# A two-branch attention block: the fourth query tile's turning transfer in two pieces, and the sums of exponentials scaled with one tensor input

## The chip, the cores and the metric

The kernel runs on one core of one Trainium2 chip. The metric is the device time of one execution in microseconds (us), from the first to the last thing that the core does. A core has a matrix engine (TensorE, PE in the profile), whose weight loads are shown apart (PEld), a vector engine (VectorE, DVE), an engine for functions of single elements (ScalarE, ACT), a general engine (GpSimd, POOL) and one that issues transfers (SyncE, SP). Transfers run on 16 DMA engines. Every transfer of this kernel is issued by SP, one after the other.

## What is computed

The reference is one decoder layer with two attention branches beside each other, cut here to what the change concerns (512 tokens behind 16 learned ones, 16 heads in each branch, all in float32):

```python
def attend(qb, qpos, cq=None):                     # one block of 128 queries
    s = jnp.einsum('bhqd,bhkd->bhqk', qb, k) * scale
    if cq is not None:                             # the second branch: forget gates, summed up
        s = s + (cq[..., :, None] - cum[:, :, None, :])
    s = jnp.where(key_pos[None, :] <= qpos[:, None], s, -jnp.inf)
    p = jax.nn.softmax(s, axis=-1)
    return jnp.einsum('bhqk,bhkd->bhqd', p, v)
...
o_mla = causal_block_attention(q_m, k_m, v_mla, MLA_SCALE)
y_mla = (o_mla * jax.nn.silu(z_mla)) @ w_br_mla
o_fox = causal_block_attention(fox_heads(fq), fox_heads(fk), fox_heads(fv), FOX_SCALE, cum)
y_fox = (o_fox * jax.nn.silu(z_fox)) @ w_br_fox
mixed = (jax.nn.sigmoid(gate_a) * y_mla + jax.nn.sigmoid(gate_b) * y_fox) @ w_out
return (h + rmsnorm(mixed, post_norm_g))[:, N_META:]
```

## The kernel before

**The whole.** First the tokens are normalised and turned, and the small projections are made. Then comes the attention in 16 stages, and then gates, branch products and the output product. Products are made in two or three passes over high and low halves of the numbers, so that they come out near float32.

**A stage.** A stage handles two heads of one branch: `stages` (L1121) goes over eight pairs of heads, FoX (`br` 1) and MLA (`br` 0) in turn. Stages are counted from 0 here, so the even ones are FoX. What a stage does is in `attention` (L938):

- `scores()` (L985): TensorE makes the scores of the four query tiles b = 0 to 3 (128 queries each, tile b with 144 + 128 b keys). VectorE takes them out of PSUM with mask or bias and row maximum (L979), and ScalarE makes the exponentials in place, each with its row sum in `su` (L1014).
- `norm(0)` for tiles 0 to 2 and `norm(1)` for tile 3 (L1021): `inverse` (L1017) multiplies the sums by 1/512 and takes reciprocals (`ri`). GpSimd writes the 16 learned tokens' probabilities (L1034 to L1039), ScalarE the high halves of the others (L1049), VectorE the low halves (L1053), all in float16 into `pn`. One transfer for each tile then turns it (keys to the partitions) into `pt` (L1072). Tile b has 2b + 3 columns of tiles, each for two heads, so the four transfers move 6, 10, 14 and 18 squares of 128 by 128.
- `values()` (L1079): 26 matmuls of `pt` by the turned values `vp` into one bank: two for the learned tokens (512 queries wide), then six for each key block j of 0 to 3, over the queries from 128 j on.

**How stages overlap.** The order of TensorE's work is the order in which the program is written (the manual schedule of L725). The loop at L1248 writes the scores of a stage, then `values()` of the stage before (`late`), then the projections for the next stage (`fill`: `fq`, `fk`, `v`, `z`, `mq`, `mk`), with `norm` written in between. So while TensorE goes through some 20 us of projections, the other engines and the transfers bring the probabilities of the stage to their place, and `values()` stands behind the next stage's scores. VectorE, ScalarE, GpSimd and SP get their order from the scheduler of the language, by priorities and dependences. It also spreads the transfers over eight completion semaphores in turn.

**SP's queue around it.** Beside the turning transfers it has the weight loads of coming stages (`wraw`), the bias rows (`cbp`), the stored and reloaded rotary part of the queries (`qpe_dram`, `QP`) and the turning of the values (`vp`). `dma` (L95) issues all of them through the same queue.

The lines that the change touches are in `inverse` and in the last loop of `norm`'s `fn`:

Of the kernel before, what the change touches and what calls it, by code (L numbers as in the profile page):

```python
# [17 lines left out]
ALU = mybir.AluOpType  # L18
# [22 lines left out]
PSCALE = 512.0  # L41
# [15 lines left out]
def block_kernel(ctx: ExitStack, tc: tile.TileContext, x, meta_tokens, pre_norm_g, w_in, fox_forget_b,  # L57
                 mla_q_norm_g, mla_kv_norm_g, w_uq, w_ukv, w_br_mla, w_br_fox, w_out, post_norm_g,
                 rope_tok, rope_pe, out):
    nc = tc.nc  # L60
# [21 lines left out]
    su = const.tile([128, 64], F32, tag="su", name="su")  # L82
# [12 lines left out]
    def dma(out, src, start=None):  # L95

        with tc.issue_after(sums_out[0]) if written[0] and sums_out else nullcontext():
            ins = (start or nc.sync.dma_start)(out=out, in_=src)
        if written[0]:
            tc.keep_in_program_order(ins)  # L100
        return ins.ins
# [300 lines left out]
    with ExitStack() as ph:  # L402
# [294 lines left out]
        with tc.issue_after(lowered[("k", 1, 0), 1]):  # L697
            nc.vector.tensor_tensor_scan(out=fa[:, 0], data0=fa[:, 1], data1=fa[:, 2], initial=0.0, op0=ALU.add,
                                         op1=ALU.add)
# [8 lines left out]
    def gate_unit(room=None, own=False):  # L708

        i, br = gates.pop(0)  # L710
        off = (O_GA, O_GB)[br]
        w, act = (plain_w(off, i), both_act) if own else (win_w(off, i, room), u_act)

        def done(_, ps):
            if len(ths) % 7 > 4:
                ths[i, br] = thx[0].tile([128, S], F32, tag="thx", name=f"th{i}{br}")
            else:
                ths[i, br] = thp.tile([128, L], F32, tag="th", name=f"th{i}{br}")[:, 0:S]
            nc.scalar.activation(ths[i, br], ps, AF.Tanh, scale=w.r)
        return unit(f"pg{i}{br}", w, act, KD, REAL, done)  # L720


    with ExitStack() as att:
# [31 lines left out]
        pn = [ac.tile([128, n, 2, 128], F16, tag=f"pn{g}", name=f"pn{g}") for g, n in enumerate((17, 9))]  # L755

        ptt = ac.tile([128, 18, 512], F16, tag="pt", name="pt")
# [8 lines left out]
        masks, normed, whole, turned_p, between = [], [], [], [], []  # L766
# [171 lines left out]
        def attention(br, pr):  # L938
# [18 lines left out]
            def sf_of(h, b):  # L957
                o, n = SF_STEP * (b % 3), 144 + 128 * b
                return sfs[b // 3][:, h, o : o + n]
# [12 lines left out]
            def evict(places):  # L972
                for b, c0, w, o, ps in places:
                    for h in range(2):
                        nb = sums["nb"][:, h, b : b + 1]
                        for a, e, in1 in added(h, b, c0, c0 + w):

                            with tc.high_priority(offset=100):
                                ins = nc.vector.tensor_tensor_reduce(  # L979
                                    out=sf_of(h, b)[:, a:e], in0=ps[h][:, o + a - c0 : o + e - c0],  # L980
                                    in1=in1, scale=-scale, scalar=3.0e38 if a == 0 else nb,
                                    op0=ALU.add, op1=ALU.min, accum_out=nb)
                return ins.ins
# [25 lines left out]
            def exponentials(bs):  # L1009
                with tc.high_priority(offset=60):  # L1010
                    for b in bs:
                        for h in range(2):
                            sf = sf_of(h, b)
                            exps[b // 3] = nc.scalar.activation(sf, sf, AF.Exp, bias=sums["nb"][:, h, b : b + 1],  # L1014
                                                                scale=-1.0, accum_out=sums["su"][:, h, b : b + 1]).ins

            def inverse(su, ri):  # L1017
                nc.vector.scalar_tensor_tensor(out=su, in0=su, scalar=1.0 / PSCALE, in1=su, op0=ALU.mult, op1=ALU.min)
                return nc.vector.reciprocal(ri, su).ins  # L1019

            def norm(g):  # L1021
                def fn():
                    b0, nb_ = GRP[g][0], len(GRP[g])
                    su, ri = (sums[t][:, :, b0 : b0 + nb_] for t in ("su", "ri"))
                    if not (three_first and g):
                        inv = inverse(su, ri)
                    if three_first and g == 0:
                        with tc.issue_after(inv):
                            evict([p_ for p_ in places if p_[0] == 3])

                    mt = aw.tile([128, 2, nb_, META], F32, tag=f"mt{g}", name=f"mt{nm_}{g}", bufs=1)
                    src = sfs[g][:, :, 0 : SF_STEP * nb_].rearrange("p h (b c) -> p h b c", b=nb_)[:, :, :, 0:META]
                    dst = pn[g][:, 0 : PN_STEP * nb_].rearrange("p (b t) h c -> p h b t c", b=nb_)[:, :, :, 0]
                    nc.gpsimd.tensor_tensor(out=mt, in0=src, in1=ri.unsqueeze(3).broadcast_to([128, 2, nb_, META]),  # L1034
                                            op=ALU.mult)
                    hi, lo, hi2 = (dst[:, :, :, 32 * i : 32 * i + META] for i in range(3))
                    nc.gpsimd.tensor_copy(hi, mt)
                    lead[:] = lead[-1:] + [nc.gpsimd.tensor_tensor(out=lo, in0=mt, in1=hi, op=ALU.subtract).ins]
                    nc.gpsimd.tensor_copy(hi2, mt)  # L1039
                    def parts(b, h):  # L1040
                        sf = sf_of(h, b)[:, META:].rearrange("p (j c) -> p j c", c=128)
                        t0 = PN_STEP * (b % 3) + 1
                        hi, lo = (pn[g][:, t0 : t0 + 2 * b + 2, h].rearrange("p (j l) c -> p j l c", l=2)[:, :, i]
                                  for i in range(2))
                        return sf, hi, lo, sums["ri"][:, h, b : b + 1]

                    def high(b, h):
                        sf, hi, _, rib = parts(b, h)
                        normed[:] = [nc.scalar.activation(hi, sf, AF.Copy, scale=rib).ins]  # L1049

                    def lower(b, h):
                        sf, hi, lo, rib = parts(b, h)
                        nc.vector.scalar_tensor_tensor(out=lo, in0=sf, scalar=rib, in1=hi, op0=ALU.mult, op1=ALU.subtract)  # L1053

                    early = three_first and g == 0
                    for b in GRP[g]:
                        if early and b == GRP[g][-1]:
                            for h in range(2):
                                high(b, h)
                            with tc.issue_after(normed[0]):  # L1060
                                exponentials((3,))
                            inv = inverse(*(sums[t][:, :, 3:4] for t in ("su", "ri")))
                            with tc.issue_after(inv):
                                for h in range(2):
                                    lower(b, h)
                            continue
                        for h in range(2):
                            high(b, h)
                            lower(b, h)
                    for b in GRP[g]:  # L1070
                        t0, n = PN_STEP * (b % 3), 2 * b + 3
                        turned_p[:] = [dma(ptt[:, 0 : 2 * n, 128 * b : 128 * b + 128], pn[g][:, t0 : t0 + n].rearrange("p t h c -> p (t h c)"),  # L1072
                                           nc.sync.dma_start_transpose)]
                        if between and b == 1:
                            with tc.issue_after(turned_p[0]):
                                between.pop()()
                return fn
# [62 lines left out]
        g = gate_unit(own=True)  # L1140
# [209 lines left out]
    with ExitStack() as mg:  # L1350
# [169 lines left out]
        for i in range(HK):  # L1520
            at, n = False, 0
# [190 lines left out]
```

## Time and profile before

| | |
|---|---|
| median of 3 runs | 580.1 us (579.19 to 581.66) |
| the profiled execution: its time | 580.54 us |
| its span, first to last instruction | 578.8 us |
| granted TensorE clock | 0.995 |
| TensorE busy | 563.0 us of the span, 3864 matmuls |
| VectorE, ScalarE, GpSimd busy | 468.0, 390.8, 232.1 us |
| moved by the DMA engines | 97.74 MB in 220025 packets |

The profile shows one execution on the chip. Times are us from the span's start, durations of single instructions are ns where a column says so. In a row such as `L104 PE MATMUL ov<-pt,vp`, L104 is the line of the kernel (here a helper through which all matmuls go), and `ov<-pt,vp` names what is written and read, without buffer numbers. In a timeline the bracket at a row's end is the engine's idle time before it and what ended it; neighbouring instructions of one kind stand in one row (x4). SPq is SP's queue: its times are those of issuing, not of moving. In the chain of waits each row starts at the time in its first column, and a row `DMA pt<-pn` reaches from the issue of a transfer to its landing.

### The profile page before, as it was taken

The numbers are of one execution on the slowest core, as the hardware profiler recorded it, in microseconds if no ns is written. First come the engines' busy times: TensorE is split into PE (matmuls) and PEld (weight loads), VectorE is DVE, ScalarE is ACT, GpSimd is POOL, SyncE is SP. The second block draws the span as 40 slices with busy tenths as digits, with TensorE's granted clock in tenths as the row PEclk, the third lists the DMA queues.
The fourth block names the chain that finished last, engine by engine and source line by source line (L and its number), as shares of the span: only waits on it lengthen the run. The fifth ranks groups of instructions, "written<-read, shape, count | busy, mean of one in ns | idle before, by whom it ended". The sixth has DMA issues, their size and how long they took to land.

```text
span 578.8 us, 11317 instructions
## 1 busy us (share of the span) xinstructions
PE 563.0 (97%) x3864; PEld 399.8 (69%) x3864; DVE 468.0 (81%) x1251; ACT 390.8 (68%) x859; POOL 232.1 (40%) x346
## 2 busy tenths in 40 slices
PE   8999979999999999999999999999999999999995
PEld 6888656667568668567676676645686675788884
DVE  6868798888878989878888788879958986478966
ACT  7867787787885886976887878864443463343762
POOL 4422823775685597756846756600000000000000
PEclk9999998999999999999999999999999999999999
DMA  8525899889999897997997986658824230323603
GB/s 301 106 56 152 254 175 290 161 210 241 193 223 220 156 200 132 217 228 150 244 247 162 211 183 146 156 102 295 286 74 110 72 110 11 110 99 109 219 0 145
DMA packets 220025, 97.74 MB, mean 169 GB/s; under 512 B 131352, under 2 KB 209568, under 8 KB 219968
## 3 DMA queue, kind: packets, MB, share of 16 engines
q1 hardware_dynamic: 219968, 97.03, 70.1%
q8 instruction: 30, 0.49, 0.3%
q14 instruction: 27, 0.22, 0.1%
HBM read 62.62 MB, written 4.23 MB: 116 GB/s over the span
## 4 chain that ended last, share of the span: by engine, by line
PE 77%; DVE 8%; DMA 5%; ACT 4%; issue 2%; POOL 2%; SPq 1%; DVEq 0%; ACTq 0%; POOLq 0%
PE z L104 15%; PE pg L104 10%; PE py L104 8%; PE fq L104 7%; PE v L104 7%; PE x L104 6%; PE fk L104 6%; PE st L104 5%; PE ov L104 5%; DMA pt<-pn 4%; PE psm L104 2%; PE mq L104 2%; PE y L104 2%; DVE w L269 1%; DVE wl L110 1%
## 5 line engine op out<-in xcount | busy, mean ns | idle before, releaser
L104 PEld LDWEIGHTS <-w 128*128 128x128 f16 x1584 | 150.1, 98 | 114.6 <-issue 4.3
L1014 ACT ACTIVATE sf<-sf,nb 128x272 f32<-128x272 f32 (+3 forms) x128 | 72.7, 568 | 25.3 <-DVE nb L979 23.1
L104 PE MATMUL z<-hTh,w 128*128 128x512 f16 x256 | 81.9, 380 | 0.0
L272 POOL TENSOR_TENSOR w<-wraw,w 128x1024 f16<-128x1024 f32 x35 | 74.9, 2141 | 2.3
L104 PE MATMUL pg<-hTh,w 128*128 128x512 f16 x240 | 72.6, 379 | 0.8 <-DVE w L269 0.8
L1053 DVE SCALAR_TENSOR_TENSOR pn<-sf,ri,pn 128x512 f16<-128x512 f32 (+3 forms) x128 | 70.9, 611 | 1.6 <-ACT pn L1049 1.6
L219 POOL TENSOR_SCALAR sc<-sc,su 128x2 f32<-128x2 f32 (+2 forms) x22 | 8.3, 379 | 146.3 <-DVE sc L216 146.3
L258 ACT ACTIVATE w<-wraw,sc 128x1024 f16<-128x1024 f32 x43 | 48.3, 1144 | 24.2 <-DVE sc L218 18.5
L1049 ACT ACTIVATE pn<-sf,ri 128x128 f16<-128x128 f32 (+3 forms) x128 | 59.6, 547 | 0.5 <-DVE ri L1019 0.5
L104 PE MATMUL z<-hTl,w 128*128 128x512 f16 x128 | 48.5, 379 | 0.0
L110 DVE TENSOR_TENSOR wl<-wraw,w 128x512 fp32r<-128x512 f32 (+1 forms) x44 | 38.4, 880 | 12.2 <-PE scale L104 4.4
L271 POOL TENSOR_SCALAR wraw<-wraw,sc 128x1024 f32<-128x1024 f32 x35 | 39.8, 1136 | 20.5 <-ACT w L258 19.4
L104 PE MATMUL pg<-hTl,w 128*128 128x512 f16 x120 | 45.5, 379 | 0.0
L104 PE MATMUL st<-hlk,hlq 64*128 64x272 f32 (+4 forms) x480 | 41.4, 299 | 0.0
L104 PE MATMUL fk<-hTh,w 128*128 128x272 f16 (+1 forms) x224 | 40.1, 276 | 0.0
L104 PE MATMUL v<-hTh,w 128*128 128x272 f16 (+1 forms) x224 | 39.3, 276 | 0.0
L104 PE MATMUL ov<-pt,vp 128*64 128x512 f16 (+4 forms) x416 | 33.2, 311 | 4.7 <-DMA pt<-pn 4.7
L104 PEld LDWEIGHTS st<-hlk,hlq 64*128 64x128 f32 x480 | 33.1, 186 | 5.8 <-ACT vh L903 2.5
L104 PE MATMUL fq<-hTh,w 128*128 128x512 f16 x112 | 35.2, 386 | 0.0
L104 PEld LDWEIGHTS <-vp 128*64 128x64 f16 (+1 forms) x416 | 22.3, 111 | 17.7 <-issue 6.9
L1415 ACT CAST w<-wraw 128x512 fp32r<-128x512 f32 x28 | 16.7, 617 | 23.1 <-DVE wraw L1424 18.6
L165 ACT CAST w<-wraw 128x1024 fp32r<-128x1024 f32 (+1 forms) x20 | 20.2, 1015 | 17.0 <-PE py L104 15.3
(342 smaller groups left out, 1478.5 us busy)
## 6 DMA issues: line engine op xcount, KB each, us to landing
wraw<-in_w_in_dram SPq DMA_DIRECT2D x47, 512.0 KB
room<-in_w_in_dram SPq DMA_DIRECT2D x9, 512.0 KB
cbp<-c_dram SPq DMA_DIRECT2D x16, 264.0 KB
wraw<-in_w_br_fox_dram SPq DMA_DIRECT2D x8, 512.0 KB
tb<-in_w_out_dram SPq DMA_DIRECT2D x8, 512.0 KB
wraw<-in_w_br_mla_dram SPq DMA_DIRECT2D x8, 512.0 KB
wraw<-in_w_out_dram SPq DMA_DIRECT2D x6, 512.0 KB
QP<-qpe_dram SPq DMA_DIRECT2D x8, 256.0 KB
```

Of the source, the lines that this page charges most:

```text
L104: nc.tensor.matmul(*a, **k)
L110: return eng.tensor_tensor(out=lo, in0=src, in1=f32(hi), op=ALU.subtract)
L165: nc.scalar.copy(wh[:, :n], raw[:, :n])
L219: nc.gpsimd.tensor_scalar(out=r, in0=t, scalar1=su[:, 5:6], scalar2=1.0, op0=ALU.mult, op1=ALU.mult)
L258: self.hi = nc.scalar.activation(hi, raw, AF.Copy, scale=self.s).ins
L269: nc.vector.scalar_tensor_tensor(out=lo, in0=raw, scalar=self.s, in1=hi, op0=ALU.mult, op1=ALU.subtract)
L271: nc.gpsimd.tensor_scalar(out=raw, in0=raw, scalar1=self.s, scalar2=1.0, op0=ALU.mult, op1=ALU.mult)
L272: nc.gpsimd.tensor_tensor(out=lo, in0=raw, in1=hi, op=ALU.subtract)
L1014: exps[b // 3] = nc.scalar.activation(sf, sf, AF.Exp, bias=sums["nb"][:, h, b : b + 1], scale=-1.0, accum_out=sums["su"][:, h, b : b + 1]).ins
L1049: normed[:] = [nc.scalar.activation(hi, sf, AF.Copy, scale=rib).ins]
L1053: nc.vector.scalar_tensor_tensor(out=lo, in0=sf, scalar=rib, in1=hi, op0=ALU.mult, op1=ALU.subtract)
L1415: nc.scalar.copy(to[0], src)
```

## The change

There are two edits, both in `attention`.

```diff
             def inverse(su, ri):
-                nc.vector.scalar_tensor_tensor(out=su, in0=su, scalar=1.0 / PSCALE, in1=su, op0=ALU.mult, op1=ALU.min)
+                su_ = su.rearrange("p h b -> p b h")
+                nc.vector.tensor_scalar(out=su_, in0=su_, scalar1=1.0 / PSCALE, scalar2=None, op0=ALU.mult)
                 return nc.vector.reciprocal(ri, su).ins
...
                     for b in GRP[g]:
                         t0, n = PN_STEP * (b % 3), 2 * b + 3
-                        turned_p[:] = [dma(ptt[:, 0 : 2 * n, 128 * b : 128 * b + 128], pn[g][:, t0 : t0 + n].rearrange("p t h c -> p (t h c)"),
-                                           nc.sync.dma_start_transpose)]
+                        for t, m in ((0, 5), (5, 4)) if b == 3 else ((0, n),):
+                            turned_p[:] = [dma(ptt[:, 2 * t : 2 * (t + m), 128 * b : 128 * b + 128],
+                                               pn[g][:, t0 + t : t0 + t + m].rearrange("p t h c -> p (t h c)"), nc.sync.dma_start_transpose)]
```

**The transfer.** Tile 3's 18 squares go in two transfers, a first piece of 10 (learned tokens and key blocks 0 and 1) and a second of 8 (key blocks 2 and 3). That is 16 more transfers in the kernel. What waited for the last turning transfer (`turned_p`) now waits for the second piece.

In the FoX stages and in stage 1 the two pieces stand where the one transfer stood. SP's queue in stage 4, before; `pn_757` is tile 3's buffer, and the last figures are partitions x squares x columns:

```order
L1103 DMA cbp_745<-c_dram 128x528
L98 DMA_TRANSPOSE pt<-pn_756 128x6x128
L98 DMA_TRANSPOSE pt<-pn_756 128x10x128
L98 DMA_TRANSPOSE pt<-pn_756 128x14x128
L98 DMA_TRANSPOSE pt<-pn_757 128x18x128
L98 DMA wraw_2354<-in_w_in_dram 128x8x128
```

and now (SP's queue, the same place):

```order
L1105 DMA cbp_745<-c_dram 128x528
L98 DMA_TRANSPOSE pt<-pn_756 128x6x128
L98 DMA_TRANSPOSE pt<-pn_756 128x10x128
L98 DMA_TRANSPOSE pt<-pn_756 128x14x128
L98 DMA_TRANSPOSE pt<-pn_757 128x10x128
L98 DMA_TRANSPOSE pt<-pn_757 128x8x128
L98 DMA wraw_2359<-in_w_in_dram 128x8x128
```

Only the last transfer of the four is cut, and nothing else moves.

In the seven MLA stages from stage 3 on, the scheduler had put tile 3's transfer second. SP's queue in stage 5, before:

```order
L98 DMA QP<-qpe_dram 128x512
L98 DMA_TRANSPOSE pt<-pn_756 128x6x128
L98 DMA_TRANSPOSE pt<-pn_757 128x18x128
L98 DMA_TRANSPOSE pt<-pn_756 128x10x128
L98 DMA_TRANSPOSE pt<-pn_756 128x14x128
L98 DMA wraw_3082<-in_w_in_dram 128x8x128
```

and now (SP's queue in stage 5):

```order
L98 DMA QP<-qpe_dram 128x512
L98 DMA_TRANSPOSE pt<-pn_756 128x6x128
L98 DMA_TRANSPOSE pt<-pn_757 128x10x128
L98 DMA_TRANSPOSE pt<-pn_756 128x10x128
L98 DMA_TRANSPOSE pt<-pn_756 128x14x128
L98 DMA_TRANSPOSE pt<-pn_757 128x8x128
L98 DMA wraw_3089<-in_w_in_dram 128x8x128
```

The second piece has moved behind tiles 1 and 2. Outside of the turning transfers the order of every engine's instructions is as it was. TensorE gains a wait: the 15th of the 26 matmuls of `values()`, the first of key block 2, waits for the second piece; the first matmul waits for the others.

**The sums.** The instruction that scales `su` read it as two tensors (times 1/512, then the minimum with itself, which is the same as the product, the sums being positive). It now reads it once, and walks it with the tiles outside and the heads inside (3 by 2 elements for tiles 0 to 2, and 2 elements for tile 3). There are 32 of them, as before.

## The prediction

> **What bounds the kernel now.** I read the page first, its table of engines and its chain of waits:
>
> ```profile
> PE 563.0 (97%) x3864; PEld 399.8 (69%) x3864; DVE 468.0 (81%) x1251; ACT 390.8 (68%) x859; POOL 232.1 (40%) x346
> ...
> PE 77%; DVE 8%; DMA 5%; ACT 4%; issue 2%; POOL 2%; SPq 1%; DVEq 0%; ACTq 0%; POOLq 0%
> ```
>
> TensorE is busy for 97% of the span and carries 77% of the chain. Nothing in the change takes work off it, so the change can gain only where TensorE waits. The waits of TensorE, longest first (sum in us, how often, the longest), say how much that is:
>
> ```profile
> PE ov L104 <- DMA pt<-pn: 4.7, 4, 2.4
> PE spun L104 <- DVE KPL L371: 1.5, 1, 1.5
> PE pg L104 <- DVE w L269: 0.8, 2, 0.4
> ```
>
> The largest wait is the one that the change touches: `values()` waits for the turning transfers, in 4 of 16 stages, 4.7 us together. All others are short and elsewhere. So 4.7 us is the most that the split can win if nothing else moves. The chain of waits in order of time shows the four places, and TensorE's timeline what each costs:
>
> ```profile
> 80.21 6.31 DMA pt<-pn
> ...
> 142.63 5.86 DMA pt<-pn
> ...
> 243.39 5.86 DMA pt<-pn
> ...
> 284.06 5.17 DMA pt<-pn
> ```
>
> ```profile
> 86.66 2.66 PE L104 MATMUL ov<-pt,vp 80*64 80x512 f16 x26 [2.42 <-DMA pt<-pn]
> ```
> ```profile
> 148.63 2.04 PE L104 MATMUL ov<-pt,vp 80*64 80x512 f16 x26 [0.86 <-DMA pt<-pn]
> ```
> ```profile
> 249.39 1.87 PE L104 MATMUL ov<-pt,vp 80*64 80x512 f16 x20 [0.70 <-DMA pt<-pn]
> ```
> ```profile
> 289.37 2.04 PE L104 MATMUL ov<-pt,vp 80*64 80x512 f16 x26 [0.76 <-DMA pt<-pn]
> ```
>
> These are stages 0, 3, 8 and 10. In each the last transfer of the stage lands (80.21 + 6.31 = 86.52, and so on) 0.14 us before the first matmul starts. In the other twelve stages TensorE finds its probabilities there.
>
> How busy the transfers are, by stretches (us, busy time of PE, PEld, DVE, ACT, POOL with counts, clock, DMA share, GB/s):
>
> ```profile
> 62.00:370.00 308.00, 302.40 (x2425) 206.10 (x2424) 256.63 (x866) 242.16 (x568) 202.80 (x293) 0.99 0.94 201
> 370.00:579.00 209.00, 201.45 (x1088) 142.78 (x1085) 165.19 (x248) 102.78 (x167) 5.52 (x14) 0.99 0.41 125
> ```
>
> In the attention the DMA engines are as full as TensorE (share 0.94), behind it not at all (0.41). So the transfers of a stage form a burst that runs at the DMA engines' pace, and the end of that burst meets `values()`.
>
> **The split, in the nine stages where the pieces stand last** (0, 8 and 10 of those that wait). SP's queue has the four transfers of a stage in one row, here stages 2, 3 and 8:
>
> ```profile
> 115.97 7.89 SPq L98 DMA_TRANSPOSE pt<-pn  x4
> ```
> ```profile
> 136.26 8.08 SPq L98 DMA_TRANSPOSE pt<-pn  x4
> ```
> ```profile
> 237.82 9.36 SPq L98 DMA_TRANSPOSE pt<-pn  x4
> ```
>
> The four move 48 squares and are issued in 7.89 to 9.36 us, 0.164 to 0.195 us a square. From the first issue to the last landing stage 3 takes 148.49 - 136.26 = 12.23 us, 0.255 a square with all latencies. So the eight squares of the second piece are worth 8 x 0.164 = 1.3 to 8 x 0.255 = 2.0 us. By so much the first piece lands earlier than the whole did; I take the lower end, since a burst's pace is nearest to its issues.
>
> What must have landed for the first matmul is now only tiles 0 to 2 and the first piece. The 15th matmul waits for the second. How long TensorE works until then I read in stage 3, whose `values()` starts at 148.63:
>
> ```profile
> 148.63:149.98 1.35, 1.35 (x15) 0.97 (x17) 1.00 1.00 99
> ```
>
> The stretch of 1.35 us holds 14 matmuls and the start of the 15th. So `values()` may start up to 1.35 us before the second piece is there. If that lands when the whole did, the gain is up to 1.3 us in a stage, and each later microsecond of the second piece eats one.
>
> What the extra transfer costs on its way: no row shows a turning transfer of 8 squares. The nearest are those of 6 to 18 squares, and the turning of the values, 9 squares:
>
> ```profile
> L98 SPq DMA_TRANSPOSE pt<-pn x64: 1210/1672/3794, 72.3 to 380.0; - x64
> ```
> ```profile
> L98 SPq DMA_TRANSPOSE vp<-vh x16: 1337/2656/4302, 65.3 to 369.4; - x16
> ```
>
> An issue takes 1.21 to 4.30 us (minimum, median, maximum in ns). But SP waits in it while the queues ahead are full, so the long ones are time that the transfers need anyway. What is new lies between nothing, if the burst is bound by its squares, and one shortest issue of 1.21 us, if it is bound by SP. I take 0.3, near nothing, since the issues follow each other without a gap while the last transfer lands 5.17 to 6.31 us behind the beginning of its own issue: the queue is behind, not SP. So the second piece lands 0.3 later than the whole did, and the gain is 1.3 - 0.3 = 1.0 us where the wait was longer.
>
> Stage 0 waited 2.42: gain 1.0. Stages 8 and 10 waited 0.70 and 0.76: both go whole.
>
> **The split, in the seven MLA stages where the second piece moves to the end** (3 of those that wait). There tile 3 stood second and tile 2 last. Tile 2 now has 40 squares up to its end and not 48, and lands 1.3 us earlier; the second piece ends the burst 0.3 later than tile 2 did, within the 1.35. Stage 3 waited 0.86: it goes whole. Behind the moved piece in the queue stand only loads for stages to come (`wraw`, `QP`), for which TensorE never waits; they move by the 0.3, in all 16 stages 5 us of queue, spread over 308 us.
>
> **The sums.** All 32 instructions, in ns, and the two rows that tell of the longest of them, on VectorE and GpSimd in stage 0:
>
> ```profile
> L1018 DVE SCALAR_TENSOR_TENSOR su<-su x32: 162/166/866, 67.6 to 371.2; 128x6 f32<-128x6 f32 x16, 128x2 f32<-128x2 f32 x16
> ```
> ```profile
> 67.58 0.87 DVE L1018 SCALAR_TENSOR_TENSOR su<-su 128x6 f32<-128x6 f32 x1 [1.13 <-ACT sf L1014]
> ```
> ```profile
> 67.14 2.53 POOL L110 TENSOR_TENSOR gT<-pt,gT 128x512 fp32r<-128x512 f32 x2
> ```
> ```profile
> L892 DVE TENSOR_SCALAR vsc<-vsc x16: 153/154/155, 59.2 to 363.2; 128x1 f32<-128x1 f32 x16
> ```
>
> A scaling with one tensor takes 154 ns on a single element, so a new one saves 0.01 us of 0.166, on an engine that TensorE does not wait for here: nothing. The exception is stage 0, where the instruction takes 866 ns while GpSimd reads two tensors. SP's first row of that stage's burst:
>
> ```profile
> 72.34 4.32 SPq L98 DMA_TRANSPOSE pt<-pn  x2
> ```
>
> If the 866 ns are a wait for a shared way into memory that one reading avoids, the reciprocals of stage 0 come 866 - 166 = 700 ns earlier, and its burst could start that much sooner. That is worth 0 to 0.70 us. I take 0: the two first issues there last 4.32 us in place of 2 x 1.21, so the queue was full in any case.
>
> The Trainium skill (SBUF — State Buffer, Who interferes with whom) has it that a VectorE instruction with two SBUF inputs and a GpSimd one that reads SBUF exclude each other for a whole instruction; the 866 ns agree. But it also says (VectorE: DVE Perf Modes, Mode 2×_2P) that a float32 `tensor_scalar` between SBUF tensors takes both ports when the outermost counts are even, or equal for source and destination, as 3 and 3 are here; by that the new instruction is held just as long, and the term is 0 too.
>
> **The sum.** 1.0 + 0.86 + 0.70 + 0.76 = 3.3 us. I take off 0.2 for a wait that comes back in a stage which now just has none, since TensorE arrives up to 3 us earlier: 3.1. The profiled execution took 580.54 us, 1.7 more than its span, and 0.4 more than the median of the runs; so 577.4 for it and 580.1 - 3.1 = **577.0** for the median. Once the attention is over the gain stays: behind 370 us TensorE is busy for 201.45 of 209.00, and what it then waits for follows from its own products.
>
> **Rivals.**
>
> *The burst does not follow.* If the DMA engines set the pace of the whole attention, TensorE gains once and waits again further on, and only stage 0's microsecond stays, with some 0.2: -1.2, 578.9. For it speaks the share of 0.94. The burst of stage 2 in the same view:
>
> ```profile
> 117.00:125.00 8.00, 8.00 (x56) 4.94 (x56) 5.83 (x17) 6.83 (x12) 6.47 (x4) 1.00 1.11 233
> ```
>
> In a burst the share is 1.11, so 0.94 is not full. Against this rival speaks too that a burst begins with probabilities, and these with TensorE's own scores: what TensorE does earlier brings the burst forward.
>
> *The fifth transfer is dear, and the kernel gets slower.* If the second piece pays like the longest turning of 9 squares, 4.30 us, in place of its share of 1.3 in the whole, it lands 3.0 later, 1.35 of it covered by the first 14 matmuls: 1.65 us more in each of the four waiting stages, +6.6, 586.7. It decides from 2.1 us on: (2.1 - 1.35) x 4 = 3 us. For it speaks the median of 2.66 us for those 9 squares. Against it, that the 48 squares with four issues take 7.89 us: 1.97 us for each transfer with its squares, so the fixed part of one is well below.
>
> The Trainium skill speaks for this rival (DMA: Bandwidth & Descriptors, Anatomy of one DMA, and the rule to coalesce small transfers): it fits about 2.0 us fixed for each transfer, on GpSimd's path. An estimate by it, with 2.0 - 1.35 = 0.65 in four stages, is +2.6 us, 582.7.
>
> *The held sum counts as well.* If one reading is not held and stage 0's burst does start 0.7 earlier: -3.8, 576.3. That the queue was full speaks against it.
>
> That the change doesn't do what it says is no rival here: the order shows the pieces and the wait for the second.
>
> **How the numbers follow.** The forecast has a chance of 0.55, the burst that does not follow 0.27, the dear transfer 0.11, the held sum 0.07. A measurement of this kernel can tell about 0.5% from no change, 2.9 us. The forecast lies just beyond that: I count 0.44 of its 0.55 as faster, 0.11 as the same. The second case is the same (0.27), the third slower (0.11), of the fourth 0.06 is faster and 0.01 the same. Faster 0.50, same 0.39, slower 0.11. The range goes down to all waits gone, 580.1 - 4.7 = 575.4, and a little for the spread of the median, 575.2. Upwards it takes in the second case with the runs' spread of about 1.3 on its 578.9: 580.2. It leaves out the dear transfer.
>
> **What would show it.** In the profile after: TensorE's wait `ov <- pt` gone in stages 3, 8 and 10 and about 1.4 in stage 0; the wait, if any, partly within the 26 matmuls and not ahead of them. SP's row of a stage with x5, not over 1.2 us longer than with x4. L1018's successor at 150 to 170 ns, in stage 0 still held. Other rows of `ov <- pt` in stages that had none would be the first rival, long waits ahead of the 15th matmul the second. Wrong would be a time over 580.2, or one under 575.2, which this wait cannot give.

## The result, and the profile after

The median went from 581.19 us (21 runs) to 579.03 us (21 runs). The ratio is 0.9962, with a 95% interval of 0.9946 to 0.9978: 2.2 us faster, 1.3 to 3.1. One of the 21 runs of after took 1159.08 us, twice the others, and is not in the ratio. Forecast were 3.1 us and a time of 577.0, in a range of 575.2 to 580.2. So the sign and the range held, and about a third of the gain is lacking. Of the 2.0 us by which the time lies over 577.0, 1.1 is the kernel before itself, which the forecast took at 580.1 from three runs. The profiled execution of after has a span of 578.3 us.

The waits of TensorE in the profile after (sum in us, how often, the longest):

```profile
PE ov L104 <- DMA pt<-pn: 2.9, 2, 1.5
PE spun L104 <- DVE KPL L371: 1.5, 1, 1.5
PE scale L104 <- ACT junk L201: 1.2, 2, 1.0
PE pg L104 <- DVE w L269: 0.7, 2, 0.4
```

The row that the change was made for fell from 4.7 to 2.9 us. A row that had 0.2 us before stands third: TensorE waits 1.2 us to sum up the scale of a weight, whose peak ScalarE (`junk`) has not found yet. TensorE's timeline at the first matmuls of `values()` in stages 0, 3, 8 and 10:

```profile
86.53 2.04 PE L104 MATMUL ov<-pt,vp 80*64 80x512 f16 x26 [1.47 <-DMA pt<-pn]
...
146.97 2.04 PE L104 MATMUL ov<-pt,vp 80*64 80x512 f16 x26 [0.16 <-PE st L104]
...
247.04 2.04 PE L104 MATMUL ov<-pt,vp 80*64 80x512 f16 x26
...
288.82 2.13 PE L104 MATMUL ov<-pt,vp 80*64 80x512 f16 x26 [1.42 <-DMA pt<-pn]
```

Stage 0 waits 1.47 and not 2.42, stages 3 and 8 no longer wait for a transfer, and stage 10 waits 1.42 where it waited 0.76. No wait stands within the 26 matmuls: the first piece covers the second. SP's queue in stages 2, 3 and 8 now has five transfers in a row:

```profile
115.07 8.47 SPq L98 DMA_TRANSPOSE pt<-pn  x5
...
135.90 8.68 SPq L98 DMA_TRANSPOSE pt<-pn  x5
...
236.63 9.64 SPq L98 DMA_TRANSPOSE pt<-pn  x5
```

They take 0.28 to 0.60 us longer than the four took. The scaling of the sums, all 32 and the one of stage 0, in ns and then in us:

```profile
L1019 DVE TENSOR_SCALAR su<-su x32: 169/172/873, 68.9 to 370.8; 128x6 f32<-128x6 f32 x16, 128x2 f32<-128x2 f32 x16
```
```profile
68.89 0.87 DVE L1019 TENSOR_SCALAR su<-su 128x6 f32<-128x6 f32 x1 [1.13 <-ACT sf L1014]
```

With one reading it takes as long as with two, 172 ns in the median, and 873 ns in stage 0. The wait that the forecast did not have is in stage 9; it makes up 0.98 us of that third row. Here are ScalarE and TensorE there, in the kernel before:

```profile
258.66 1.06 ACT L201 ACTIVATE junk<-wraw 128x1024 bf16<-128x1024 f32 x1 [0.51 <-DMA wraw<-in_w_in_dram]
```
```profile
260.72 0.17 PE L104 MATMUL scale<-sc,spread 128*128 128x2 bf16 x1
```

And the same two in the kernel after:

```profile
258.31 1.06 ACT L201 ACTIVATE junk<-wraw 128x1024 bf16<-128x1024 f32 x1 [0.56 <-DMA wraw<-in_w_in_dram]
```
```profile
259.51 0.16 PE L104 MATMUL scale<-sc,spread 128*128 128x2 bf16 x1 [0.98 <-ACT junk L201]
```

After, ScalarE is done at 258.31 + 1.06 = 259.37, and 0.14 us later TensorE goes on, having stood there since 258.53. Before, ScalarE was done at 259.72, so that TensorE could have gone on at 259.86; it came at 260.72. That is a margin of 0.86 us, and so no wait. Now TensorE comes 2.2 us sooner and the weight only 0.35 us: 2.19 - 0.35 - 0.86 = 0.98.

The granted clock of TensorE differs too. The same 4 us behind stage 0's wait, before and then after (us, busy time of PE and its matmuls, granted clock, DMA share, GB/s):

```profile
87.50:91.50 4.00, 4.00 (x26) 0.57 1.09 308
```
```profile
87.50:91.50 4.00, 4.00 (x34) 1.00 1.01 300
```

Before, the trace has TensorE at half its clock for 3.41 us, from 87.91 to 91.32; after, it has no such stretch within the attention. The forecast, which counts waits alone, has no term for this.

### The profile page after: what moved, and what is told of

Same layout as the page of the kernel before. It is cut to its first block, busy times and chain, and to the rows that moved or that the text cites. A ratio compares the mean times of both kernels' runs of the same rounds, so it can differ in the third digit from the quotient of the medians.

```text
span 578.3 us, 11369 instructions
## 1 busy us (share of the span) xinstructions
PE 563.0 (97%) x3864; PEld 401.1 (69%) x3864; DVE 467.3 (81%) x1251; ACT 390.4 (68%) x859; POOL 232.0 (40%) x346
## 4 chain that ended last, share of the span: by engine, by line
PE 69%; DVE 9%; ACT 3%; DMA 2%; issue 1%; DVEq 0%; POOL 0%; ACTq 0%; POOLq 0%
PE z L104 15%; PE pg L104 10%; PE py L104 8%; PE x L104 6%; PE v L104 6%; PE st L104 5%; PE fk L104 5%; PE fq L104 5%; PE ov L104 4%; PE mq L104 2%; PE y L104 2%; DMA wraw<-in_w_in_dram 1%; DVE sc L203 1%; DVE w L269 1%; DVE wl L110 1%
```

## The experiments

Two theories in turn. The first: the split does all of it, and what is lacking is lost in stage 10, whose transfers stand in SP's queue behind the load of `QP`, and that behind stores to DRAM. The second was formed after the first eight runs: it is lost at the weight of stage 9. Their common rival is that the DMA engines' pace over the whole attention is the limit, so that each wait taken away comes back elsewhere. All ratios are against the kernel before.

**The split alone.** In the kernel after, the scaling is put back:

```diff
-                su_ = su.rearrange("p h b -> p b h")
-                nc.vector.tensor_scalar(out=su_, in0=su_, scalar1=1.0 / PSCALE, scalar2=None, op0=ALU.mult)
+                nc.vector.scalar_tensor_tensor(out=su, in0=su, scalar=1.0 / PSCALE, in1=su, op0=ALU.mult, op1=ALU.min)
```

> The split without the new form of the scaling. First theory (the split does it all): the same as the whole change, ratio 0.996 (-2.2 us), the waits of TensorE for the probabilities 2.9 us as after it. Rival (the scaling with one reading carries a part): nearer to 1, 0.998 or above, and the waits longer than 2.9 us.

Measured: 0.9955 [0.9937, 0.9973]. Its longest waits:

```profile
PE scale L104 <- ACT junk L201: 2.1, 2, 1.9
PE ov L104 <- DMA pt<-pn: 1.7, 2, 1.3
```

The whole gain is here without the new scaling. `scale <- junk` is longer still, 1.9 us of it in stage 9.

**One reading alone.** The same exchange the other way round, in the kernel before.

> The new form of the scaling without the split. First theory: no change, ratio 1.000, waits of 4.7 us as before, the scaling still about 870 ns long in stage 0. Rival (it carries a part): 0.998 or below.

Measured: 0.9998 [0.9977, 1.0020]. Its first waits:

```profile
PE ov L104 <- DMA pt<-pn: 6.4, 4, 2.2
PE spun L104 <- DVE KPL L371: 1.5, 1, 1.5
```

The edit does nothing. The 6.4 us, in place of 4.7, show how far one execution's waits lie from another's in kernels of the same time. There is no wait for a peak in stage 9.

**The stores cut, in the kernel after and in the one before.** The two heads that the next load of `QP` reads are stored first and each by itself:

```diff
-                for i in range(2):
-                    dma(qpe_dram[8 * g + a : 8 * g + b, i, x], results(x)[16 * a : 16 * b, i])
+                for h0, h1 in ((a, a + 1), (a + 1, a + 2), (a + 2, b)):
+                    for i in range(2 if h1 > h0 else 0):
+                        dma(qpe_dram[8 * g + h0 : 8 * g + h1, i, x], results(x)[16 * h0 : 16 * h1, i])
```

> The whole change, and the stores of the rotary part to DRAM are cut, so that the two heads that the next load of QP reads go first and each by itself (16 rows of 2 KB), the other heads behind them. First theory (stage 10's burst of transfers stands behind that load in SP's queue, and the load behind the stores, which take 3.5 to 4.3 us): the stores that the load waits for land in about 2 us, the load is issued 2 us or more earlier, stage 10's wait of 1.42 us goes, that of stage 0 shrinks by up to 1 us: waits of 1 us or less in all, ratio 0.992 to 0.994. Rival (the pace of the DMA engines over the whole attention is the limit): the waits come back elsewhere, ratio 0.996 as with the change alone, 2.5 to 3 us of waits. Third case (more issues cost SP time): above 0.996.

> The kernel before with the cut stores alone. First theory: stage 10's wait of 0.76 and stage 8's of 0.70 us go, stage 0's 2.42 shrinks by up to 1, stage 3's 0.86 stays: -1.5 to -2.5 us, ratio 0.996 to 0.9975. Rival (pace of the DMA engines as a whole): 0.999 to 1.000 with waits of about 4.7 us. Third case (more issues): above 1.

Measured: 1.0087 [1.0060, 1.0115] and 1.0122 [1.0095, 1.0150], 5.0 and 7.1 us slower. The third case, then. Waits of the first of the two, and SP's queue in its stage 0:

```profile
PE ov L104 <- DMA pt<-pn: 3.4, 3, 1.8
PE scale L104 <- ACT junk L201: 2.8, 2, 2.6
PE st L104 <- issue: 2.6, 1, 2.6
```
```profile
68.73 6.65 SPq L98 DMA_DIRECT2D qpe_dram<-gT  x12
75.50 3.30 SPq L98 DMA_TRANSPOSE pt<-pn  x2
79.40 0.37 SPq L98 DMA_DIRECT2D QP<-qpe_dram  x1
```

Twelve stores take 6.65 us to issue, 0.55 each. The load of `QP` comes later, and TensorE stands 2.6 us ahead of scores that read it. In both, TensorE also waits 2.6 us for the weight of stage 9, without the split too. A part of the loss goes with the clock: its mean is 0.9905 and 0.9898 in these runs, and 0.9951 in the runs of the kernel before beside them, which over 580 us is an estimated 2.7 and 3.1 us. These runs change too much at once to try the theory; they show that SP has little time for further issues in stages 0 and 8.

**One pair of stores cut.** Only the pair right ahead of stage 10's load of `QP`, first in the kernel after, then in the kernel before:

```diff
-                for i in range(2):
-                    dma(qpe_dram[8 * g + a : 8 * g + b, i, x], results(x)[16 * a : 16 * b, i])
+                heads = ((a, a + 1), (a + 1, a + 2), (a + 2, b)) if g and x and b == 8 else ((a, b),)
+                for h0, h1 in heads:
+                    for i in range(2 if h1 > h0 else 0):
+                        dma(qpe_dram[8 * g + h0 : 8 * g + h1, i, x], results(x)[16 * h0 : 16 * h1, i])
```

> The whole change, and only the one pair of stores right ahead of stage 10's load of QP is cut (four of 16x512 first, two of 4x16x512 behind them, in place of two of 6x16x512). First theory (stage 10's transfers stand behind the load of QP, and that behind the stores): QP issued 3 us or more sooner after the stores, stage 10's wait of 1.42 us gone and none new in stages 11 to 15, -1.4 us beside the change: ratio 0.993 to 0.9945, about 577.6 us against 581.2. Rival (the DMA engines' pace over the whole attention): the wait comes back further on, ratio 0.996. Third case (four more issues cost as much as they free): a wait of about 1 to 2.6 us for a weight (scale <- junk) in stage 9 or 10, ratio 0.996 to 1.000.

> The kernel before with the same one pair of stores cut, without the split. First theory: stage 10's wait of 0.76 us goes, those of stages 0, 3 and 8 (2.42, 0.86, 0.70) stay: ratio 0.998 to 0.9995. Rival (pace of the DMA engines): ratio 1.000, the wait in stage 10 or a later one.

Measured: 0.9949 [0.9929, 0.9969] and 0.9988 [0.9971, 1.0005]. SP's queue at the end of stage 9, in the kernel after and then with the pair cut:

```profile
266.43 1.48 SPq L98 DMA_DIRECT2D qpe_dram<-gT  x2
272.37 0.35 SPq L98 DMA_DIRECT2D QP<-qpe_dram  x1
```
```profile
267.02 3.15 SPq L98 DMA_DIRECT2D qpe_dram<-gT  x6
270.35 0.37 SPq L98 DMA_DIRECT2D QP<-qpe_dram  x1
...
272.44 5.58 SPq L98 DMA_TRANSPOSE vp<-vh  x1
...
279.27 9.13 SPq L98 DMA_TRANSPOSE pt<-pn  x5
```

The load of `QP` had stood 4.46 us behind the last store's issue (266.43 + 1.48 = 267.91 to 272.37); with the cut it stands 0.18 behind the last, and 1.37 behind the fourth (done at 268.98), the last that it reads. So SP's queue did hang on the stores. But the transfers of stage 10 begin at 279.27, and at 279.43 in the kernel after: the turning of the values, which stands between, now takes 5.58 us. Stage 10 waits 0.45 us in the kernel after with the cut, 2.01 in the kernel before with it. The time with the cut cannot be told from that of the change alone, and the interval of the kernel before with it holds both 1 and what the first theory forecast. So the hold is real, but that it costs the lacking part is not borne out; the first theory falls for good with the runs below.

**One more cut of the second piece.**

```diff
-                        for t, m in ((0, 5), (5, 4)) if b == 3 else ((0, n),):
+                        for t, m in ((0, 5), (5, 2), (7, 2)) if b == 3 else ((0, n),):
```

> The whole change, with the second piece cut once more (10, 4 and 4 squares): the price of one more transfer in each of 16 stages, the first piece unchanged. First theory (a further transfer makes the end of a burst 0.3 us later, which the matmuls on the first piece cover): as with the change alone, ratio 0.996, waits of 2.9 us, issue row of a stage with x6 not over 1.2 us longer. Rival (a transfer has a high fixed price): the third piece lands 1.5 to 2 us later, waits within the 26 matmuls in four or more stages, ratio above 0.998.

Measured: 1.0129 [1.0089, 1.0169], 7.5 us slower than before and some 10 slower than with two pieces. Its longest waits, and the row of stage 1 in SP's queue, then that row in the kernel after:

```profile
PE ov L104 <- DMA pt<-pn: 9.8, 5, 3.8
PE scale L104 <- ACT junk L201: 2.9, 2, 2.7
```
```profile
96.81 12.85 SPq L98 DMA_TRANSPOSE pt<-pn  x6
```
```profile
95.27 11.16 SPq L98 DMA_TRANSPOSE pt<-pn  x5
```

The burst of stage 1 begins 1.54 us later and takes 1.69 longer, and stage 1 waits 3.8 us, where it did not wait at all. The rival has the sign right, though the wait lies mostly ahead of the matmuls (1.86 of the 9.8 us, in stage 10, lie within): the price is paid by what stands behind in the queue. The mean clock of these runs is 0.9938, against 0.9978 after, an estimated 2.3 of the 10 us.

**The scaling not held.** The first scaling of stage 0 also writes a sum, into a number that is no longer read:

```diff
-                nc.vector.tensor_scalar(out=su_, in0=su_, scalar1=1.0 / PSCALE, scalar2=None, op0=ALU.mult)
+                nc.vector.tensor_scalar(out=su_, in0=su_, scalar1=1.0 / PSCALE, scalar2=None, op0=ALU.mult,
+                                        **(dict(op1=ALU.add, accum_out=sums["nb"][:, 0, 0:1]) if free else {}))
```

> The whole change, and the first scaling of stage 0 in the form that also writes a sum over its row, into a number no longer needed. By the Trainium skill (SBUF, Who interferes with whom) this form does not take the shared ports: the scaling of stage 0 lasts about 0.17 to 0.25 us in place of 0.87. Theory of the prediction (stage 0's queue is full in any case, the 0.7 us are worth nothing): first transfer of the probabilities of stage 0 no or up to 0.4 us earlier, wait of stage 0 1.2 to 1.5, ratio 0.996. Rival (the held sum counts): stage 0's wait 0.7 us shorter, ratio 0.9945 to 0.995.

Measured: 0.9972 [0.9954, 0.9990]. The scaling in stage 0, and the first transfers of the probabilities:

```profile
67.63 0.17 DVE L1019 TENSOR_SCALAR_CACHE_REDUCE su<-su 128x6 f32<-128x6 f32 x1 [1.13 <-ACT sf L1014]
```
```profile
71.90 4.73 SPq L98 DMA_TRANSPOSE pt<-pn  x2
```

`free` is true for that one alone. It takes 0.17 us and not 0.87, so the hold is off. The transfers begin 4.27 us behind its start, 0.5 us sooner than after (68.89 to 73.66: 4.77); but the two issues last 4.73 in place of 4.38, the next begin at 77.81, and stage 0 waits 1.61 us. As far as these runs tell, the held sum is worth nothing with the split as well.

**The stores behind the weight loads.** At the end of stage 8 two stores stand in SP's queue ahead of the three weight loads of which the last is late in stage 9. They are moved behind these and the turning of the values, and nothing else in SP's queue or in TensorE's order moves:

```diff
-                if 8 <= si < 10:
+                if si == 9:
                     written[0] = True
                     with tc.issue_after(turned_p[0]):
-                        store1(si - 8, 2, 8)
+                        store1(1, 2, 8)
                     written[0] = False
...
                     run(loads_of(sets[si]))
+                if si == 9:
+                    written[0] = True
+                    with tc.issue_after(loaded[0]):
+                        store1(0, 2, 8)
+                    written[0] = False
```

> The whole change, and the two stores that stand ahead of three weight loads in SP's queue at the end of stage 8 (two of 6x16x512) moved behind these loads and the turning of the values. Second theory, formed from the runs so far (in all kernels with the split TensorE waits 0.8 to 1.9 us for a weight's peak in stage 9, scale <- junk, in none without it, and the last of these three loads lands at about the same time in both: the part of the gain that is lacking goes there, and the loads are late because the stores use 6 of the 16 DMA engines ahead of them): the last load lands 1.5 to 3 us sooner, the wait scale <- junk of stage 9 goes, -1 us or more beside the change, ratio 0.9925 to 0.994. Rival (the loads are late for another reason, the room that GpSimd sets free or the turnings ahead of them): the wait stays, ratio 0.996. Third case (the stores then hold the transfers of stage 9): a wait for the probabilities of 1 to 3 us in stage 9, ratio 0.997 to 1.000.

Measured: 577.24 us, 0.9922 [0.9897, 0.9946], 4.5 us faster than before. This is, with the next, the fastest of all versions. SP's queue at the end of stage 8, after and then with the stores moved:

```profile
246.33 1.57 SPq L98 DMA_DIRECT2D qpe_dram<-gT  x2
248.01 5.54 SPq L98 DMA_DIRECT2D wraw<-in_w_in_dram  x3
```
```profile
244.05 3.12 SPq L98 DMA_DIRECT2D wraw<-in_w_in_dram  x3
247.27 2.47 SPq L98 DMA_TRANSPOSE vp<-vh  x1
249.79 1.57 SPq L98 DMA_DIRECT2D qpe_dram<-gT  x2
...
262.29 1.48 SPq L98 DMA_DIRECT2D qpe_dram<-gT  x2
268.09 0.35 SPq L98 DMA_DIRECT2D QP<-qpe_dram  x1
```

ScalarE and TensorE at the weight of stage 9, with the stores moved:

```profile
253.76 1.06 ACT L201 ACTIVATE junk<-wraw 128x1024 bf16<-128x1024 f32 x1
```
```profile
256.88 0.17 PE L104 MATMUL scale<-sc,spread 128*128 128x2 bf16 x1
```

The three loads are issued in 3.12 us and not in 5.54. ScalarE finds the last one there (no bracket in its row) and is done at 254.82, 2 us ahead of TensorE. Neither stage 9 nor stage 10 waits; the row for the probabilities is down to 0.8 us, all in stage 0. The wait of the second theory is gone, and the time came. But this profile is of the fastest of the six runs (575.88 us), and not all of its lead comes from the move: TensorE reaches stage 0's `values()` 1.34 us sooner than after and waits 0.66 less there, both ahead of the moved stores. And stage 10 does not wait although the load of `QP` stands behind its stores as long as ever (262.29 + 1.48 = 263.77 to 268.09: 4.32 us).

**Both edits.** The move of the stores and the one pair cut.

> The kernel of the run before with the stores behind the weight loads, and with the pair of stores ahead of stage 10's load of QP cut as well (four of 16x512 first, two of 4x16x512 behind). Second theory: waits of stages 9 and 10 both gone, what is left is stage 0's and stage 1's: ratio 0.991 to 0.993. Rival (pace of the DMA engines): no more than either edit alone, 0.994 to 0.996.

Measured: 0.9924 [0.9901, 0.9947], as with the move alone. The cut adds nothing. Its waits for the probabilities:

```profile
PE ov L104 <- DMA pt<-pn: 3.6, 4, 1.3
```

As with the move alone, TensorE does not wait for the weight of stage 9. But stages 0, 1, 8 and 10 wait 1.33, 0.71, 0.58 and 1.01 us, so the move does not take these waits away, as the one profile of the run before could make believe. And stage 10 waits here although the load of `QP` now stands 1.57 us behind the stores: its wait does not go by that hold.

**The move in the kernel before.** The same move, without the split.

> The kernel before with the two stores moved behind the weight loads, without the split. Second theory: in the kernel before nothing waits for this weight, TensorE arrives 1 us or more after it is ready, so the move gains nothing: ratio 0.999 to 1.001. Rival (the move helps by itself, as the stores hold the loads and turnings of stage 9 in both): 0.9975 or below.

Measured: 0.9971 [0.9948, 0.9994]. That is where the rival had it (0.9975 or below) and not where the second theory had it (0.999 to 1.001), though the interval just reaches that. Its waits:

```profile
PE ov L104 <- DMA pt<-pn: 5.0, 3, 2.5
```

Of these 5.0 us, 2.48 are in stage 0, 0.21 in stage 1 and 2.27 in stage 8, all ahead of the moved stores; stage 10 waits another 0.10, where the other three kernels without the split wait 0.76 to 2.10. So the move seems to gain some 1.7 us by itself, by another way than the weight of stage 9, for which nothing waits here; by which, one profile does not show. With the move in both, the split takes 0.9971 to 0.9922: about 2.9 us, against 2.2 without the move. If the wait in stage 9 cost the change its whole length, the two would lie that much apart; the 0.7 us by which they do is not told from nothing, nor from 1.5, by these intervals.

**The change once more.** The kernel after, unaltered.

> The change once more, unaltered, for a second profile: which of its waits belong to the program and which to one execution. Second theory (the lacking part goes to the weight of stage 9): scale <- junk of 0.8 to 2 us in stage 9 again, ratio 0.9945 to 0.998. First theory (it goes to stage 10's transfers behind QP): stage 10 waits about 1.4 us again, and stage 9 not necessarily. If stage 10 comes out below 0.7 us, the 1.42 us of the first profile was one execution's, as the 0.1 to 0.45 us of the other kernels with the split let one expect.

Measured: 0.9976 [0.9956, 0.9996]. Its first two waits:

```profile
PE ov L104 <- DMA pt<-pn: 2.6, 3, 1.6
PE scale L104 <- ACT junk L201: 2.1, 2, 1.9
```

Stage 9 waits again, 1.88 us of the second row. Stage 10 waits 0.93, and 0.10, 0.34 and 0.45 in the split alone, with the scaling not held and with one pair cut. Stage 9's wait, in all five profiles, is the program's. Stage 10's 1.42 us is the longest of five, but 0.93 is not under the 0.7 that was to show it as one execution's alone; how much of it is the program's stays open.

## Why the prediction was right, and where it was not

**The waits that the split takes: right in sum, a little less.** Forecast were 3.3 us less at `values()`. Four kernels without the split waited there 4.7, 6.4, 6.1 and 5.0 us, five profiles with it and with stage 8's stores in their place show 2.9, 1.7, 3.2, 3.0 and 2.6: 5.55 and 2.68 in the mean, 2.9 us less (the kernels with all stores cut and with three pieces are left out). With the waits at the same place that the profile puts down to TensorE's own scores (0.16, 0.34 and 0.93, in the first, third and last of the five) it is 2.6 us less. Single stages are less sure than the prediction took them to be: stage 8, read as 0.70, waited 1.5, 1.4 and 2.3 in the other three without the split, stage 3 not at all. Stage 10, whose wait was to go, waits in all five with it, 0.10 to 1.42 us. Stage 1, which waits in neither of the two profiles compared, waits 0.21 to 0.52 us in the other three without the split, and 0.38 to 1.22 in three of the five with it.

**Stage 0: right.** 1.47 was measured for about 1.4, and 1.28 to 1.63 in the other four of these five.

**The price of the extra transfer: right; its ground does not carry further.** The sixteen rows of turning transfers in SP's queue take 136.0 us together in the mean of the four profiles without the split and 141.2 in the five with it: 0.32 us a stage, for the 0.3 that was taken. The ground given was that SP runs ahead of a full queue, so that an issue more costs little. That would hold for a sixth as well, but with three pieces the rows take 163.0 us, 1.36 more a stage, about one shortest issue. What differs stands in the single issues of tile 3 in the FoX stages. The 18 squares whole take 3.2 to 3.3 us in the mean of a profile, and the 10 and the 8 together 3.2 to 3.4: the whole was as dear as its pieces. The 8 squares take 1.4 to 1.6 us, cut into 4 and 4 they take 2.7. Why 18 squares are so dear in one issue stays open. The dear transfer, given 0.11, is thus no matter of the fifth but of the sixth.

**The sums: right.** Zero was taken and 0.9998 measured. The Trainium skill's rule (VectorE: DVE Perf Modes, Mode 2×_2P), that the new form takes both ports, agrees with the 873 ns in stage 0. By the Trainium skill (SBUF — State Buffer, Who interferes with whom) the form which also writes a sum does not; its 0.17 us agree.

**The step that failed: the 0.2 for a wait that comes back.** No row stood behind the 0.2. The nearest ground is the sentence that behind the moved piece stand only loads for stages to come, "for which TensorE never waits". It was said of the seven MLA stages, but it fails behind stage 8's burst: TensorE waits for the third weight load there. It stood at 0.98, 1.91, 0.79, 1.78 and 1.88 us in the five profiles with the split: 1.5 us in the mean, not 0.2. In the four without the split it does not occur; the kernel before with all stores cut has it. From the first matmul of `values()` in stage 8 to that in stage 9 TensorE takes 20.26 or 20.27 us in each of the six profiles without this wait, two of them with the split and the move, and 21.2 to 22.3 us in the five with it. So the wait lengthens TensorE's way there by its whole length.

The margin of 0.86 us could be read in the two rows of before shown above; a list of waits does not show it. Two other profiles without the split have 0.80 and 1.17. Over all the profiles with stage 8's stores in place it is also not TensorE alone that moved: it comes 1.3 us sooner in the mean with the split, and the weight is ready 1.1 us later.

**The term that the sum does not have: the clock.** "4.7 us is the most that the split can win" leaves out what follows a long wait. Each of the four profiles without the split has one stretch of 3.41 us at half clock within the attention. It begins 1.0 to 1.4 us behind a wait of 2.01 to 2.48 us; three waits of 2.13 to 2.27 us there have none behind them. The seven with two pieces and at most one pair of stores cut, whose longest wait is 1.91 us, have no such stretch. What one costs shows where it lies behind stage 10, as with one reading alone:

```profile
291.00:293.00 2.00, 2.00 (x17) 0.50 1.15 345
```

In the two such profiles TensorE takes 100.18 us from the first matmul of `values()` in stage 10 to that in stage 15, and 98.54 to 98.65 in the other nine of these eleven: 1.6 us more. Not every run has such a stretch. The mean granted clock is 0.9951 in 23 runs of the kernel before, taken beside the split alone, and 0.9978 in 20 of after; 0.0027 of 580 us is an estimated 1.6 us. Beside the second measurement of the change it is 0.9955 and 0.9968, an estimated 0.8. That shorter waits are what keeps the clock up is argued from which profiles have the stretches; no run changes the one without the other.

**The sum.** 2.6 us of waits and 1.6 of the clock, less 1.5 for the weight, are 2.7; timed were 2.2 (1.3 to 3.1). In the second measurement 2.6 + 0.8 - 1.5 = 1.9 stand against 1.4. So the forecast's 3.1 came as near as it did partly by luck: of two terms of 1.5 us that it had at 0.2 and not at all, one makes up for the other. By the prediction's own mark of 2.9 us, under which a change counts as the same, the outcome is the same (0.39) and not faster (0.50).

**The rivals.** The burst that does not follow was right in that a gain is waited for again further on: the weight of stage 9 is ready no sooner although TensorE is. Its 1.2 us lie about as near to the 2.2 that were timed as the forecast's 3.1, and nearer to the 1.4 of the second measurement. About the cause it was wrong for that wait: with two stores moved and no byte less to carry the weight is there in time in both profiles, so it was the order in the queue and not the DMA engines' pace over the whole attention. For the waits that are left at the probabilities no run shows which it is. The held sum is out by two runs.

## What to carry to other kernels

When an engine is let arrive earlier, list not only its waits but what it meets next without one, and subtract: when the supply is ready, when the engine comes. Here margins of 0.8 to 1.2 us turned into waits of 0.8 to 1.9. Look at the granted clock behind the longest waits too: a wait of over 2 us that goes can take a stretch at half clock with it, and then it was worth more than its length. And look in the same queue for what stands ahead of the late supply and is needed later than it: moving two stores brought as much again as the change, though not all of that by the wait for which they were moved.

## What the runs showed of the hardware

- Cutting a turning transfer is not free or dear as such. 18 squares in one issue took SP as long as 10 and 8 apart (3.2 to 3.3 and 3.2 to 3.4 us in the means of the FoX stages); but no issue, not even one of 4 squares, went below 1.19 us, as the row of the kernel with three pieces shows (ns), and one more in each stage cost the kernel 10 us. The Trainium skill (DMA: Bandwidth & Descriptors, Anatomy of one DMA) gives about 2.0 us fixed for a transfer on GpSimd's path; the fifth transfer, with 0.32 us a stage in SP's queue, does not show it, the sixth, with 1.36, does in its direction.

```profile
L98 SPq DMA_TRANSPOSE pt<-pn x96: 1194/1425/4434, 72.3 to 392.9; - x96
```

- Behind two stores of 6x16x512 the load that needs them was issued 4.46 us after the last one's issue, behind four of 16x512 1.37 us. The Trainium skill (DMA: Bandwidth & Descriptors, Why a DMA increments its semaphore by 16 and not by 1) has a transfer use the largest number of engines, up to 16, that divides the slowest dimension of both sides: 6 engines and 16. The two holds agree with it, but the four small stores ahead of the load also carry a third of the bytes of the two (128 KB and 384 KB), so they do not show that it is the engines.
- The same three weight loads were issued in 5.54 us behind two such stores, and in 3.12 and 2.23 us ahead of them.
- TensorE's granted clock went to half for 3.41 us, 1.0 to 1.4 us behind waits of 2.01 to 2.48 us, in four of eleven profiles. Three waits of 2.13 to 2.27 us among these have none behind them, and neither has any of 1.91 us or less.
